# Meta tokens' squares from the copy loaded for the transposes, and the first row of products in the order of its operands

## The chip, the cores and the metric

The kernel runs on one core of a Trainium2 chip. TensorE (PE) multiplies: a matmul first loads a block of stationary operand (PEld in the profile, one LDWEIGHTS), then streams the columns of the moving operand past it and adds into a PSUM bank. VectorE (DVE) and ScalarE (ACT) do elementwise work, GpSimd (POOL) fills constants and issues a few DMAs, SyncE (SP) issues most DMAs. The metric is the device time of one execution in microseconds. The kernel before takes 1206.83 us, the median of three runs from 1205.95 to 1206.94.

## The reference, cut to what matters

```python
meta_b = jnp.broadcast_to(meta[None], (B, N_META, D_MODEL))     # 16 x 2048
h = jnp.concatenate([meta_b, x], axis=1)                        # 272 tokens
u = rms_norm(h, g_pre_mix[l])        # h / sqrt(mean(h*h) + eps) * g, token by token
proj = u @ w_in[l]                   # 2048 x 7168, split into z_pool, v, g, gate_a, gate_b
# pooling of z_pool, gated causal convolution of v and g, gates, w_o, second norm,
# w_up, relu squared, w_down, third norm
return h[:, N_META:]
```

The 272 tokens are 16 meta tokens ahead of 256 tokens of x. Each token's row is scaled by the root of the mean of its 2048 squares. The kernel multiplies the unscaled rows by the weights and brings the scale in afterwards, so the sums of squares are needed only when the first products are evacuated.

## The kernel before, in words

Everything is float32. To keep that precision, each operand is split into a high part in a rounded format of 4 bytes (fp32r) and a low part, the remainder in the same format; a product is the sum of high times high, high times low and low times high. ACT writes the high parts (L259, L1011, L1397), DVE the low parts (L262, L1016, L1402). Weights come as chunks of 128 partitions by 2048 columns into a raw buffer of 8192 bytes per partition, three in rotation, and are split into the buffers `hi` and `lo`, three of each.

The stages, in the order of TensorE's work:

- **Opening** (to about 38 us): `meta` is loaded twice, once as `m_rows`, 128 rows of two pieces of 128 columns, for the transposes, and once as `m_in`, 16 rows of 2048, for the squares. The tokens are turned by TensorE (L378, L396) into `u`, 16 tiles (k) of 128 features by 272 tokens, high and low. As soon as a k is there, `product_of(k)` (L538) multiplies it into four accumulators, by `mm3` (L441, matmuls at L446): three matmuls of 272 columns for each accumulator, stationary `hi` or `lo`, moving `u`. `x_tile`, `row` and `squares_of` for later k are issued in between, by the loop at L558; this order is written by hand. `keep_warm` (L364) issues matmuls that nobody reads ahead of the first product.
- **The other products of `u` with `mm3`** (to 155 us): the rest of v and g, and z, also 272 columns.
- **Gates** (to 330 us): `block_t` (L712, matmuls at L717) with the roles exchanged: `u` from its 17th token on is stationary, `hi` and `lo` are streamed, 512 columns.
- **Group map, pool and conv outputs, w_o** (to 512 us): L446 with 256 columns, then L717 and L1055 with 512 streamed columns of weights.
- **MLP** (to the end): products up by `mm2` (L460): `mm2_high` (L451) streams 512 columns (the high and low parts of 256 tokens) of the activations, tile `m`, past a stationary `hi`; `mm2_low` (L457) streams 256 columns of `m` past a stationary `lo`. Products down (L1551) stream 512 columns of weights past stationary `forms`. The order in both w_o and the MLP is made by a planner (class Plan) from costs and due times.

**Where tiles lie.** Tiles come from pools that stand one behind the other in each partition: `const` (small constants, each rounded up to 32 bytes), `big` (named slots: a tile that asks for the tag of an earlier one shares its place, and slots stand in the order in which their tags are first asked for), `raws`, `parts` (the `hi` and `lo` buffers), `tmp`. The kernel places some tiles by units of `LINE`, 16 floats or 64 bytes: the tile `shift` of three LINEs in `const` (L302), the offset of one LINE at the head of `m` (L815) and of one of the two `forms` (L1292), and in `part_tile` (L227):

```python
place = 2 if standing and tag == "hi" else 1
shift = (place - 1 - 3 * KEYS.index(key)) % 4 * LINE
return room[:, shift:shift + CK * CW]
```

So every `hi` and `lo` starts at the same remainder of 256 bytes, except the `hi` of the products up, which starts one LINE (64 bytes) later. In `big` the tags are asked for in the order k8 (two slots), a, c, um, s1, s0. The slot of tag a holds first `m_in` and later the convolution's input (8 x 286 floats, 9152 bytes), the slot of tag um holds `u` and later `m`.

Of the kernel before, what the change touches and what calls it, by code (L numbers as in the profile page):

```python
# [8 lines left out]
F32 = mybir.dt.float32  # L9
F32R = mybir.dt.float32r  # L10
AF = mybir.ActivationFunctionType
ALU = mybir.AluOpType
PSUM = bass.MemoryType.PSUM

P = 128
CK = 4
# [84 lines left out]
def hybrid_block(ctx: ExitStack, tc: tile.TileContext, ins: dict, out: bass.AP):  # L101
    nc = tc.nc
    x = ins["x"][0]
    meta = ins["meta"]
    T, D = x.shape
    M = meta.shape[0]
    L = M + T
    NT = T // P
    KD = D // P
# [17 lines left out]
    const = ctx.enter_context(tc.tile_pool(name="const", bufs=1))  # L127
    big = ctx.enter_context(tc.tile_pool(name="big", bufs=1))
    raws = ctx.enter_context(tc.tile_pool(name="raws", bufs=3))
    parts = ctx.enter_context(tc.tile_pool(name="parts", bufs=1))  # L130
    tmp = ctx.enter_context(tc.tile_pool(name="tmp", bufs=2))
# [6 lines left out]
    def acc_tile(name):  # L138
        return psA.tile([P, CW], F32, tag="acc", name=name)
# [73 lines left out]
    opened = []  # L213
# [21 lines left out]
    def open_chunk(loads=None):  # L235

        n = at["n"]
        at["n"] += 1
        src, (rows, width) = stream[n]
        raw = raws.tile([P, CK * CW], F32, tag="raw", name=f"raw_{n}")  # L240
        hi, lo = (part_tile(tag, at["parts"], n in standing_chunks) for tag in ("hi", "lo"))
        at["parts"] += 1
        flat, (raw, hi, lo) = raw, (t.rearrange("p (k c) -> p k c", k=rows) for t in (raw, hi, lo))
        if n < FIRST:
            dst = raw.rearrange("p k (h c) -> p k h c", h=2)
            for load in loads or [(slice(i, i + 2), BOTH, nc.sync) for i in range(0, rows, 2)]:
                if callable(load):
                    load()
                    continue
                sl, halves_, queue = load  # L250
                for k in range(sl.start, sl.stop):
                    queue.dma_start(dst[:, k, halves_], src[:, k, halves_])
        else:
            nc.sync.dma_start(raw, src)
        pieces = rows if n < FIRST else 4 if n == FIRST else 1
        k = rows // pieces

        def high(sl, cs):
            nc.scalar.copy(hi[:, sl, cs], raw[:, sl, cs])  # L259

        def low(sl, cs):
            nc.vector.tensor_sub(lo[:, sl, cs], raw[:, sl, cs], f32(hi[:, sl, cs]))  # L262

        def piece(i, cs):
            def f():
                sl = slice(i * k, (i + 1) * k)
                high(sl, cs)
                low(sl, cs)
            return f
        todo = [piece(i, slice(0, width)) for i in range(pieces)]  # L270
        if n == 0:
            todo[:1] = [piece(0, slice(h * HALF_CW, (h + 1) * HALF_CW)) for h in range(2)]
        opened.append((hi, lo, todo, flat))
# [5 lines left out]
    def fetch(ahead=2):  # L279

        for c in range(ahead + 1):
            if c == len(opened) and at["n"] < len(stream):
                open_chunk()
            if c < len(opened):
                split_pieces(c)
        flush()
        return opened.pop(0)[:2]
# [13 lines left out]

    const.tile([P, 3 * LINE], F32, name="shift")  # L302
    x_in = big.tile([P, NT, D], F32, tag="k8", bufs=2, name="x_in")
    m_in = big.tile([M, D], F32, tag="a", name="m_in")
    xv = x.rearrange("(t p) d -> p t d", p=P)
    XB = D // CW

# [24 lines left out]
    def load_x(queue, b, ts=slice(0, NT), cs=(0, 2)):  # L332

        sl = slice(b * CW + cs[0] * CW // 2, b * CW + cs[1] * CW // 2)
        queue.dma_start(x_in[:, ts, sl], xv[:, ts, sl])

    m_rows = tmp.tile([P, M * KD // P, P], F32, tag="v", bufs=5, name="m_rows")
    nc.sync.dma_start(m_rows, meta.rearrange("m (k f) -> (m k) f", f=P).rearrange(  # L340
        "(h p) f -> p h f", p=P))
    pre_rows = load_rows(nc.scalar, "g_pre_mix")
# [7 lines left out]
    load_x(nc.sync, 1)  # L350
    open_chunk()
    load_x(nc.sync, 2)
    nc.sync.dma_start(m_in, meta)
    open_chunk()
    load_x(nc.sync, 3)
    other_rows = load_rows(nc.gpsimd, "pool_scale", "b_dw", "conv_ln_g", "conv_ln_b", "g_pre_mlp")
# [1 line left out]
    nc.gpsimd.dma_start(taps_in, w_dw)  # L358
    ssq = const.tile([P, NT + 1, 2], F32, name="ssq")
    nc.gpsimd.memset(ssq, 1.0)  # L360

    idle = acc_tile("idle")

    def keep_warm(n):  # L364
        for _ in range(n):
            nc.tensor.matmul(idle[:, :P], rb[:, :P], rb[:, :P], start=True, stop=True)

    keep_warm(7)

    u = big.tile([P, KD, 2, -(-L // (4 * LINE)) * 4 * LINE], F32R, tag="um", name="u")[:, :, :, :L]
# [19 lines left out]
    def x_tile(k):  # L392
        pt = misc_tile(f"xt_{k}")[:, :T]
        sl = slice(k * P, (k + 1) * P)
        for t in range(NT):
            nc.tensor.transpose(pt[:, t * P:(t + 1) * P], x_in[:, t, sl], ident)  # L396
        nc.scalar.activation(u[:, k, 0, M:], pt, AF.Copy, scale=col("g_pre_mix", k))
        nc.vector.scalar_tensor_tensor(
            u[:, k, 1, M:], pt, col("g_pre_mix", k), f32(u[:, k, 0, M:]),
            op0=ALU.mult, op1=ALU.subtract)  # L400

    def squares_of(t, b):

        sl = slice(b * D // 2, (b + 1) * D // 2)
        src, n = (x_in[:, t, sl], P) if t < NT else (m_in[:, sl], M)
        nc.scalar.activation(src, src, AF.Square, accum_out=ssq[:n, t, b:b + 1])

    def rsqrt(r, q, var):

# [31 lines left out]
    def mm3(acc, hi, lo, act, k, cs, first, last):  # L441


        off = act.shape[3] - acc.shape[1]
        for n, (w, a) in enumerate(((hi, 0), (hi, 1), (lo, 0))):
            nc.tensor.matmul(acc, w[:, k[0], cs], act[:, k[1], a, off:],  # L446
                             start=first and n == 0, stop=last and n == 2)
# [18 lines left out]
    def acc_tiles(name, n=CW // P):  # L466
        return [acc_tile(f"acc_{name}_{j}") for j in range(n)]
# [68 lines left out]
    accs = [acc[:, :L] for acc in acc_tiles("vg0")]  # L536

    def product_of(k):  # L538
        for j, acc in enumerate(accs):
            mm3(acc, *opened[k // CK][:2], u, (k % CK, k), slice(j * P, (j + 1) * P),  # L540
                k == 0, k == KD - 1)

    def row(k):
        opened[k // CK][2].pop(0)()

    def x_pair(k):

        x_tile(k)
        x_tile(k + 1)
# [4 lines left out]
    row(0)  # L554
    x_tile(1)
    row(1)
    keep_warm(6)
    for k in range(KD):  # L558
        product_of(k)
        if k % CK == CK - 1:  # L560
            open_chunk()
        if k in (0, 2):
            for kx in (k + 2, k + 3):
                x_tile(kx)
                row(kx)
        elif k % 2 == 0 and k + 3 < KD:
            x_pair(k + 2)
        elif k + 3 < KD and k > 1:
            row(k + 3)
            row(k + 4)  # L570
        squares = {4: (NT, 0), 6: (0, 0), 8: (1, 0), 10: (NT, 1)}
        if k in squares:
            squares_of(*squares[k])
        if k == KD - 5:
            row(KD)
    for _ in range(3):
        row(KD)
    for t in range(NT):
        squares_of(t, 1)
# [177 lines left out]
    hi, lo = fetch()  # L757
    for g in range(NG):
        for j in range(GK):
            q = g * GK + j  # L760
            acc = (acc_tile if q < KP - 2 else misc_tile)(f"acc_grp_{q}")[:, :T]
# [476 lines left out]
    accs = acc_tiles("up00")  # L1238
# [41 lines left out]
    hi, lo = fetch()  # L1280
# [459 lines left out]
    for e, cs in enumerate(col_halves):  # L1740
        for w, s in ends:
            h = AT[s][0]
# [53 lines left out]
```

## Time and profile before

| | |
|---|---|
| runs | 1205.95, 1206.94, 1206.83 us; median 1206.83 |
| the profiled execution | 1206.63 us, its span 1204.5 us |
| granted clock of TensorE, mean | 0.998 |
| PE busy | 1195.1 us (99% of the span), 6444 matmul records |
| PEld busy | 1038.0 us (86%) |
| DVE busy | 974.3 us (81%) |
| ACT busy | 625.2 us (52%) |
| POOL busy | 8.3 us |
| DMA | 238.40 MB, mean 198 GB/s |

The span runs from the first to the last instruction of the profiled execution; the 2.1 us by which its time exceeds the span lie around it. A row of a group says: line, engine, operation, out<-in by the program's names, shape and count, then busy time in us and the mean duration of one in ns. Matmuls are pipelined: the duration of one is longer than the distance from its start to the start of the next, and the next one's LDWEIGHTS runs beside it. A matmul of plain float32 stands in the trace as two records.

### The profile page before, as it was taken

Reading aid. Unit: us, or ns where it says so; the run is one execution under the profiler, and the core shown is the slowest. Engines: PE = TensorE matmul, PEld = TensorE weight load, DVE = VectorE, ACT = ScalarE, POOL = GpSimd, SP = SyncE. Lnnn points to the kernel's source line nnn. Section 1 sums busy time; section 2 is a strip of 40 time slices with the busy share of each in tenths; the row PEclk is TensorE's granted clock in tenths of the full one; section 3 lists DMA queues with packets and bytes.
Section 4 is the critical chain, followed back from the end, with each engine's and each line's share of the span. In section 5 each row is a group of like instructions: output and inputs, shape, how many; then the busy total and the mean of one; then the engine's idle time right before and its main releaser. Section 6 shows DMA issues by size and latency. Waiting matters only on the chain.

```text
span 1204.5 us, 15705 instructions
## 1 busy us (share of the span) xinstructions
PE 1195.1 (99%) x6444; PEld 1038.0 (86%) x6444; DVE 974.3 (81%) x1054; ACT 625.2 (52%) x633; POOL 8.3 (1%) x19
## 2 busy tenths in 40 slices
PE   9999999999999999999999999999999999999997
PEld 9999988888888888898888888888888888888886
DVE  5899978999676778678988878788878778788756
ACT  6533344443583455666555564564554555554543
POOL 1000000000000000000000000000000000000000
PEclk9999999999999999999999999999999999999999
DMA  9655555656557588546475675674764764755841
GB/s 293 210 177 179 188 193 180 205 181 203 177 172 280 174 264 260 174 167 218 143 242 175 186 233 160 196 250 140 244 200 155 262 197 152 245 175 172 278 145 70
DMA packets 162678, 238.40 MB, mean 198 GB/s; under 512 B 4161, under 2 KB 92417, under 8 KB 162080
## 3 DMA queue, kind: packets, MB, share of 16 engines
q1 hardware_dynamic: 160032, 230.77, 58.4%
q0 software_dynamic: 1680, 5.40, 1.7%
q10 hardware_dynamic: 896, 1.25, 0.3%
q8 instruction: 50, 0.82, 0.3%
q14 instruction: 20, 0.16, 0.0%
HBM read 235.30 MB, written 2.10 MB: 197 GB/s over the span
## 4 chain that ended last, share of the span: by engine, by line
PE 97%; DMA 2%; DVE 1%; ACT 0%; ACTq 0%; DVEq 0%; issue 0%
PE bank_u L451 18%; PE acc_gate L717 14%; PE acc_up L1551 14%; PE bank_u L457 9%; PE bank_a L1551 7%; PE o_c L1055 6%; PE bank_b L1551 5%; PE acc_z L446 4%; PE acc_co L717 4%; PE acc_po L717 4%; PE acc_v L446 3%; PE acc_g L446 3%; PE acc_up L451 1%; PE acc_vg L446 1%; PE bank_u L1551 1%; DMA x_in<-in_x_dram 1%
## 5 line engine op out<-in xcount | busy, mean ns | idle before, releaser
L451 PE MATMUL bank_u<-m,hi 128*128 128x512 f32 x960 | 329.9, 390 | 0.0
L457 PE MATMUL bank_u<-m,lo 128*128 128x256 f32 x960 | 265.5, 277 | 0.0
L259 ACT CAST hi<-raw 128x2048 fp32r<-128x2048 f32 (+2 forms) x94 | 151.0, 1619 | 191.6 <-PE acc_gate L717 67.7
L1402 DVE TENSOR_TENSOR lo<-raw_m,hi 128x2048 fp32r<-128x2048 f32 x85 | 194.5, 2290 | 59.4 <-ACT hi L1397 59.3
L1397 ACT CAST hi<-raw_m 128x2048 fp32r<-128x2048 f32 x85 | 162.4, 1911 | 138.1 <-PE bank_u L451 76.8
L262 DVE TENSOR_TENSOR lo<-raw,hi 128x2048 fp32r<-128x2048 f32 (+2 forms) x94 | 180.1, 1925 | 42.5 <-ACT hi L259 42.0
L451 PEld LDWEIGHTS bank_u<-m,hi 128*128 128x128 f32 x960 | 180.2, 188 | 37.9
L457 PEld LDWEIGHTS bank_u<-m,lo 128*128 128x128 f32 x960 | 180.3, 188 | 1.6
L717 PE MATMUL acc_gate<-hi,u 128*128 128x512 f32 x512 | 158.6, 390 | 0.0
L1551 PE MATMUL acc_up<-hi,forms 128*128 128x512 f32 x496 | 157.5, 389 | 0.0
L512 DVE SCALAR_TENSOR_TENSOR c<-a,taps,c 128x256 f32<-128x256 f32 x240 | 115.7, 484 | 6.8
L717 PEld LDWEIGHTS acc_gate<-hi,u 128*128 128x128 f32 x512 | 96.1, 188 | 19.9
L1551 PEld LDWEIGHTS acc_up<-hi,forms 128*128 128x128 f32 x496 | 93.1, 188 | 19.4
L717 PE MATMUL acc_gate<-lo,u 128*128 128x512 f32 x256 | 99.6, 389 | 0.0
L1551 PE MATMUL acc_up<-lo,forms 128*128 128x512 f32 x248 | 96.6, 389 | 0.0
L1402 DVE TENSOR_TENSOR lo<-raw_c,hi 128x2048 fp32r<-128x2048 f32 x29 | 66.4, 2290 | 20.9 <-ACT hi L1397 20.9
L1551 PE MATMUL bank_a<-hi,forms 128*128 128x512 f32 (+1 forms) x256 | 82.0, 383 | 0.0
L1397 ACT CAST hi<-raw_c 128x2048 fp32r<-128x2048 f32 x29 | 55.3, 1908 | 50.9 <-PE bank_u L451 27.9
L1402 DVE TENSOR_TENSOR lo<-raw_a,hi 128x2048 fp32r<-128x2048 f32 x29 | 66.4, 2290 | 17.6 <-ACT hi L1397 17.5
L1397 ACT CAST hi<-raw_a 128x2048 fp32r<-128x2048 f32 x29 | 55.4, 1910 | 42.4 <-PE bank_u L451 19.4
L1055 PE MATMUL o_c<-hi,m 128*128 128x512 f32 x208 | 65.6, 390 | 0.0
L1551 PE MATMUL bank_b<-hi,forms 128*128 128x512 f32 (+1 forms) x200 | 63.7, 382 | 0.0
(317 smaller groups left out, 1853.0 us busy)
## 6 DMA issues: line engine op xcount, KB each, us to landing
raw<-in_w_in_dram SPq DMA_DIRECT2D x52, 1024.0 KB, 5.1
raw_m<-in_w_down_dram SPq DMA_DIRECT2D x37, 1024.0 KB, 5.3
raw_m<-in_w_up_dram SPq DMA_DIRECT2D x33, 1024.0 KB, 6.1
raw_c<-in_w_down_dram SPq DMA_DIRECT2D x14, 1024.0 KB, 5.2
raw_a<-in_w_up_dram SPq DMA_DIRECT2D x13, 1024.0 KB, 6.0
raw_a<-in_w_down_dram SPq DMA_DIRECT2D x13, 1024.0 KB, 5.3
raw_c<-in_w_up_dram SPq DMA_DIRECT2D x12, 1024.0 KB, 5.8
raw_o<-in_w_o_dram SPq DMA_DIRECT2D x10, 1024.0 KB, 7.2
```

The costliest lines, as they stand in the source:

```text
L259: nc.scalar.copy(hi[:, sl, cs], raw[:, sl, cs])
L262: nc.vector.tensor_sub(lo[:, sl, cs], raw[:, sl, cs], f32(hi[:, sl, cs]))
L446: nc.tensor.matmul(acc, w[:, k[0], cs], act[:, k[1], a, off:], start=first and n == 0, stop=last and n == 2)
L451: nc.tensor.matmul(acc.rearrange("p (a t) -> p a t", a=2)[:, :, ts], hi[:, k[0], cs], act[:, k[1], :, off + ts.start:off + ts.stop], start ...
L457: nc.tensor.matmul(acc[:, :T], lo[:, k[0], cs], act[:, k[1], 0, off:], start=False, stop=stop, skip_group_check=True)
L512: nc.vector.scalar_tensor_tensor(c, conv["a"][:, q, i:i + T], taps[:, q, i:i + 1], c, op0=ALU.mult, op1=ALU.add)
L717: nc.tensor.matmul(acc, act(kk)[:, a_, ts_], w_[:, k, :], start=kk == 0 and n == 0, stop=kk == nk - 1 and n == 2)
L1055: nc.tensor.matmul(acc, form(k, a_), box[w_][:, k, :], start=start and k == 0 and n == 0, stop=stop and k == CK - 1 and n == 2, skip_group ...
L1397: nc.scalar.copy(box["flat"], raw)
L1402: nc.vector.tensor_sub(lo, raw, f32(box["flat"]))
L1551: nc.tensor.matmul(acc, forms[h][:, f, k, a_, :], box[w_][:, k, cs], start=start and k == 0 and n == 0, stop=stop and k == KH - 1 and n == ...
```

## The change

The second copy of `meta` goes: no tile `m_in`, no DMA for it, no two ACT squares over it (k = 4 and k = 10). In its place ACT squares the two 128-column pieces of `m_rows` early and sums each row (a row holds 128 of the 2048 features of one meta token) into `row_ssq`; POOL makes a mask `rows_of` that says which rows belong to which token; two matmuls on TensorE (`meta_squares`) add the rows of each token into a corner of the PSUM tile `idle`; and DVE copies those 16 sums into `ssq` at k = 1. `ssq`'s second column for the meta tokens is set to zero. `keep_warm` ahead of the first product goes from 6 to 3. In `product_of(0)` the twelve matmuls are issued operand by operand (high weights with high `u` for all four accumulators, then high with low, then low with high) instead of accumulator by accumulator.

```diff
     x_in = big.tile([P, NT, D], F32, tag="k8", bufs=2, name="x_in")
-    m_in = big.tile([M, D], F32, tag="a", name="m_in")
...
-    m_rows = tmp.tile([P, M * KD // P, P], F32, tag="v", bufs=5, name="m_rows")
+    RH = M * KD // P
+    m_rows = tmp.tile([P, RH, P], F32, tag="v", bufs=5, name="m_rows")
...
     load_x(nc.sync, 2)
-    nc.sync.dma_start(m_in, meta)
...
     nc.gpsimd.memset(ssq, 1.0)
+    nc.gpsimd.memset(ssq[:, NT, 1:], 0.0)
+
+    rows_of = const.tile([P, RH, M], F32, name="rows_of")
+    nc.gpsimd.memset(rows_of, 1.0)
+    for sign, base in ((1, 0), (-1, KD - 1)):
+        nc.gpsimd.affine_select(rows_of, rows_of, pattern=[[sign * P, RH], [-sign * KD, M]],
+                                compare_op=ALU.is_ge, fill=0.0, base=base,
+                                channel_multiplier=sign)
+    row_ssq = const.tile([P, RH], F32, name="row_ssq")
...
     keep_warm(7)
+    for h in range(RH):
+        nc.scalar.activation(tmp.tile([P, P], F32, tag="junk", bufs=1, name=f"sqm_{h}"), m_rows[:, h, :], AF.Square,
+                             accum_out=row_ssq[:, h:h + 1])
...
     def squares_of(t, b):
 
         sl = slice(b * D // 2, (b + 1) * D // 2)
-        src, n = (x_in[:, t, sl], P) if t < NT else (m_in[:, sl], M)
-        nc.scalar.activation(src, src, AF.Square, accum_out=ssq[:n, t, b:b + 1])
+        src = x_in[:, t, sl]
+        nc.scalar.activation(src, src, AF.Square, accum_out=ssq[:, t, b:b + 1])
...
     def product_of(k):
-        for j, acc in enumerate(accs):
-            mm3(acc, *opened[k // CK][:2], u, (k % CK, k), slice(j * P, (j + 1) * P),
-                k == 0, k == KD - 1)
+        hi, lo = opened[k // CK][:2]
+        if k:
+            for j, acc in enumerate(accs):
+                mm3(acc, hi, lo, u, (k % CK, k), slice(j * P, (j + 1) * P), False, k == KD - 1)
+            return
+        for n, (w, a) in enumerate(((hi, 0), (hi, 1), (lo, 0))):
+            for j, acc in enumerate(accs):
+                nc.tensor.matmul(acc, w[:, 0, j * P:(j + 1) * P], u[:, 0, a, :], start=n == 0,
+                                 stop=False)
+
+    def meta_squares():
+
+        tot = idle[:M, P:P + 1]
+        for h in range(RH):
+            nc.tensor.matmul(tot, rows_of[:, h, :], row_ssq[:, h:h + 1],
+                             start=h == 0, stop=h == RH - 1)
+        return tot
...
-    keep_warm(6)
+    keep_warm(3)
+    meta_tot = meta_squares()
...
-        squares = {4: (NT, 0), 6: (0, 0), 8: (1, 0), 10: (NT, 1)}
+        squares = {6: (0, 0), 8: (1, 0)}
         if k in squares:
             squares_of(*squares[k])
+        if k == 1:
+            nc.vector.tensor_copy(ssq[:M, NT, 0:1], meta_tot)
```

Two things follow from this for where tiles lie. `const` grows by `rows_of` (2 x 16 floats, 128 bytes) and `row_ssq` (2 floats, rounded up to 32 bytes), 160 bytes together, so all pools behind it start 160 bytes later. And tag a is first asked for only when the convolution's input is made, after c and um: its slot of 9152 bytes now stands behind um instead of ahead of c, and c and um (with `u` and `m`) move forward by 9152 - 160 = 8992 bytes. Start addresses per partition in the two programs:

| tile | before | after |
|---|---|---|
| `x_in`, first of `big` | 20544 | 20704 |
| `u`, later `m` (whose data start 64 further) | 70656 | 61664 |
| slot s1 (`forms_1`, whose data start 64 further) | 111616 | 111776 |
| slot s0 (`forms_0`) | 128064 | 128224 |
| first raw buffer | 144448 | 144608 |
| `lo`, first buffer | 169024 | 169184 |

## The prediction

> **What bounds the kernel now.** I read the page's busy times first, then the chain that ended last.
>
> ```profile
> PE 1195.1 (99%) x6444; PEld 1038.0 (86%) x6444; DVE 974.3 (81%) x1054; ACT 625.2 (52%) x633; POOL 8.3 (1%) x19
> ...
> PE 97%; DMA 2%; DVE 1%; ACT 0%; ACTq 0%; DVEq 0%; issue 0%
> ```
>
> TensorE is busy 99% of the span and carries 97% of the chain. So there are two ways to move the time: the few microseconds in which TensorE waits, and the pace at which its 6444 records follow each other. The chain in order of time gives the pace of long unbroken stretches:
>
> ```profile
> 107.99 47.36 PE acc_z L446 x384
> 155.35 144.17 PE acc_gate L717 x636
> ```
>
> A matmul of 272 columns follows the last after 47.36/384 = 123 ns, one of 512 after 227 ns. The groups kept apart by shape have their durations:
>
> ```profile
> L451 PE MATMUL bank_u<-m,hi 128*128 128x512 f32 x960 | 329.9, 390 | 0.0
> L457 PE MATMUL bank_u<-m,lo 128*128 128x256 f32 x960 | 265.5, 277 | 0.0
> ...
> L446 PE MATMUL acc_z<-u,hi 128*128 128x272 f32 x256 | 47.4, 286 | 0.0
> ...
> L446 PE MATMUL acc_grp<-d,hi 128*128 128x256 f32 x32 | 5.8, 283 | 0.0
> ```
>
> 286 - 123 = 163 ns, and for the gates 390 (the duration that the 512-column group above also has) - 227 = 163 ns: duration is pace plus a constant, so a nanosecond more of duration is one more of time. What stands out: 256 columns take 277 ns in the products up and 283 ns in the group map. The first products up, asked for line by line in short windows, show what decides:
>
> ```profile
> L451 PE MATMUL acc_up<-m,hi x16: 276/276/366, 519.1 to 520.9; 128*128 128x256 f32 x16
> L457 PE MATMUL acc_up<-m,lo x16: 282/283/283, 521.0 to 522.8; 128*128 128x256 f32 x16
> L451 PE MATMUL acc_up<-m,parts_up x16: 281/283/364, 523.3 to 525.2; 128*128 128x256 f32 x16
> L451 PE MATMUL acc_up<-m,parts_up x16: 279/279/362, 528.1 to 530.0; 128*128 128x256 f32 x16
> ```
>
> All four stream 256 columns of `m`, whose data start at 70720, remainder 64 of 256 bytes. I call *distance* the start of the stationary operand loaded meanwhile minus the start of the streamed one, modulo 256. In the first row `hi` has place 2, remainder 128: distance 64, 276 ns. Second: `lo` at 64: distance 0, 283. Third: `parts_up` in slot s0 (128064, remainder 64): distance 0, 283. Fourth: slot s1 (111616, remainder 0): distance 192, 279. In the group map `d` lies in a k8 slot (remainder 64 like `x_in`) and `hi` at 64: 0, and 283 again. So for 256 columns the distance is worth up to 7 ns a matmul.
>
> **The change part by part.**
>
> *Where tiles lie.* By the table of addresses, `hi` and `lo` with place 1 go from remainder 64 to 224, `u` from 0 to 224, the data of `m` from 64 to 32, the `hi` of products up from 128 to 32. The distances:
> - L446 with 272 columns (`u` streamed): 64 becomes 0.
> - `mm2_low` (then `hi` is loaded): 64 becomes 0.
> - `mm2_high` (then `lo` is loaded): 0 becomes 192.
> - gates and w_o (`hi`, `lo` streamed, `u` or `m` loaded): 0 becomes 64.
> - L1551, pool and conv outputs, group map: 0 stays 0.
>
> *mm2_low*: 960 x (283 - 277) = +5.8 us. The ends are 0 (the pace does not follow the address here) and +5.8.
>
> *272 columns*: 192 (vg) + 288 (v) + 288 (g) + 384 (z) = 1152 matmuls, for which no row has distance 0. Free of any loss, 256 columns take 276 ns; each further column costs (227 - 113)/256 = 0.44 ns (113 = 276 - 163), so 272 would take 283 and now lose 3. Ends: 283 (-3 ns, -3.5 us) and 286 + 7 = 293 (+8.1 us). I take the free 283 plus the 7 that distance 0 costs in the group map, the nearest row since it is the same helper: 290, +4 ns, +4.6 us.
>
> *mm2_high*: no row has 512 columns at distance 192. At 0 they take 390; at 64 they are seen only where a product down ends and `hi` of a product up is loaded:
>
> ```profile
> 573.59 0.39 PE L1551 MATMUL acc_up<-lo,forms 128*128 128x512 f32 x1
> 573.81 0.39 PE L1551 MATMUL acc_up<-hi,forms 128*128 128x512 f32 x1
> 574.04 0.40 PE L451 MATMUL bank_u<-m,hi 128*128 128x512 f32 x1
> ```
>
> The last L1551 before L451 lasts no longer than the one before. So 512 columns don't seem to feel the distance: 0 for `mm2_high`, gates and w_o. The other end for `mm2_high` comes from a stretch of the same addresses at a slower pace, against the rest of the stage:
>
> ```profile
> L451 PE MATMUL bank_u<-m,hi x31: 393/393/396, 543.2 to 553.7; 128*128 128x512 f32 x31
> ...
> L457 PE MATMUL bank_u<-m,lo x31: 281/281/281, 543.4 to 553.9; 128*128 128x256 f32 x31
> ...
> L451 PE MATMUL bank_u<-m,hi x876: 389/389/398, 599.9 to 1157.4; 128*128 128x512 f32 x176
> ...
> L457 PE MATMUL bank_u<-m,lo x877: 276/276/280, 599.8 to 1157.7; 128*128 128x256 f32 x176
> ```
>
> There 512 columns reach 396: 960 x (396 - 390) = +5.8 us. That the pace differs at equal addresses also says that it isn't the distance alone.
>
> *The offset itself*: all big tiles now start 32 bytes off the 64-byte grid. DVE and ACT already work on such a tile, `dm` (L643), in the slot of tag junk, which starts 32 off that grid:
>
> ```profile
> L1512 DVE TENSOR_TENSOR forms<-F_raw,forms 128x512 fp32r<-128x512 f32 x32 | 21.8, 685 | 0.0
> L1511 ACT CAST forms<-F_raw 128x512 fp32r<-128x512 f32 x32 | 19.5, 617 | 0.5
> ...
> L649 DVE TENSOR_TENSOR d<-dm,d 128x512 fp32r<-128x512 f32 x4 | 2.7, 684 | 0.0
> L646 ACT CAST d<-dm 128x512 fp32r<-128x512 f32 x4 | 2.4, 612 | 0.0
> ```
>
> 684 against 685 and 612 against 617 ns: nothing. TensorE has no such row; I take 0.
>
> *The opening*, from the timeline:
>
> ```profile
> 4.69 0.12 POOL L360 MEMSET ssq<- 128x6 f32 x1
> 5.71 0.47 ACT L397 ACTIVATE u<-xt,vecs 128x256 fp32r<-128x256 f32 x1 [1.99 <-PE xt L396]
> 5.80 1.50 PE L366 MATMUL idle<-rb 128*128 128x128 f32 x12
> 6.08 0.70 ACT L259 CAST hi<-raw 128x256 fp32r<-128x256 f32 x2
> 6.62 0.41 DVE L390 TENSOR_TENSOR u<-mg,u 128x256 fp32r<-128x256 f32 x1
> 6.95 0.76 DVE L262 TENSOR_TENSOR lo<-raw,hi 128x256 fp32r<-128x256 f32 x2
> 7.06 0.49 PE L446 MATMUL acc_vg<-u,hi 128*128 128x272 f32 x2
> 8.15 0.69 DVE L262 TENSOR_TENSOR lo<-raw,hi 128x512 fp32r<-128x512 f32 x1
> 8.66 0.35 SPq L353 DMA_DIRECT2D m_in<-in_meta_dram  x1
> 8.77 0.60 PE L396 MATMUL xt<-ident,x_in 128*128 128x128 f32 x4
> 9.12 0.50 PE L446 MATMUL acc_vg<-u,hi 128*128 128x272 f32 x2
> 17.42 1.06 ACT L406 ACTIVATE m_in<-m_in 16x1024 f32<-16x1024 f32 x1 [0.35 <-DMA m_in<-in_meta_dram]
> ```
>
> Row 0 now takes 7.06 to 8.77, since each accumulator waits for its low weights (ready at 7.71). In the new order four matmuls with the high `u` can start at 6.75 (three `keep_warm` fewer, 0.75 us, then some 0.2 us for the two mask products), four with the low `u` from 7.24, four with the low weights from 7.73: the next transposes start at 8.2 instead of 8.77. Row 1's low weights still come at 8.15 + 0.69 = 8.84, so its third matmul gains some 0.6 us (from 9.12 + 0.37). The two squares on ACT (some 0.5 us each) lie in the 1.99 us that it idles ahead of 5.71; with `m_rows` late they would delay `u` one for one. POOL's four extra steps (0.1 to 0.3 us each, from 4.81) end before 6; TensorE would wait for them if they took twice that. Out go 128 KB from SP's queue and ACT's square ahead of later weight rows. But the loads carry on as before:
>
> ```profile
> 8.00:10.00 2.00, 2.00 (x19) 2.00 (x18) 1.10 (x3) 0.94 (x3) 0.00 (x0) 1.00 1.04 289
> 10.00:15.00 5.00, 5.00 (x41) 4.89 (x41) 3.63 (x8) 3.34 (x9) 0.00 (x0) 1.00 1.11 355
> ```
>
> With the DMA share (next to last) at 1.04 to 1.11 a lead can be lost to the next late load. Ends: 0 and -1.1 us (0.6 plus the freed 0.5 us of transfer); I take -0.6. DVE's copy at k = 1 (some 0.2 us) lies in its idle time: 0, or 0.2.
>
> *Sum*: 5.8 + 4.6 + 0 - 0.6 = +9.8 us on the profiled 1206.63, which is 0.2 below the median 1206.83; against the median 1216.6.
>
> **The rivals.**
> 1. *Layout costs nothing, the opening alone counts*: 1206.2 us. For it: equal addresses show two paces in the products up. Against: four rows of distance 0 or 64 that agree to 1 ns. The Trainium skill, in "TensorE: Matmul & The Clock Gate", Part 2: What happens when you issue a matmul, has the next weights loaded through a read port of their own that takes nothing from the running matmul; by that rule no address matters and this rival's time would come out. The trace doesn't agree: 276 and 283 ns for the same instruction.
> 2. *512 columns pay too*: 5.8 us more, 1222.4, and with 272 columns at their upper end 1225.9. For it: the 396 ns; against: 390 and 389 wherever the distance is 0.
> 3. *Faster: distance 0 is the free one for 272 columns.* In the stages of L446 1152 x 3 ns = -3.5 us, with the opening 1202.7. It decides (below 1204.4) only if `mm2_low` loses less than 1.8 ns each. Against: 283 in the group map with the same helper.
> 4. *Half a 64-byte step costs TensorE itself*: at the same 7 ns on 6444 records, +45 us, 1251. No row for it.
>
> **How the numbers follow.** Some 0.2% (2.4 us) is what a measurement of this kernel can tell from no change. Chances: forecast 0.44 (range 1210 to 1220), rival 1 0.20, rival 2 0.20, rival 3 0.11, rival 4 0.05. Slower 0.44 + 0.20 + 0.05 = 0.69, same 0.20, faster 0.11. The range leaves out rivals 3 and 4: from 1204.5 to 1228.
>
> **What would show it.** L457 of `bank_u` at 283 instead of 277 ns; L446 `acc_z` at 290 instead of 286; L451, L717 and L1551 unchanged near 390; the second pair of transposes at 8.2 us; stage borders of the chain after 540 us drifting apart at some 5.8 us over the MLP. It is wrong if the 272- or 256-column rows keep their durations, if 512 columns change, or if TensorE waits for the mask or the row sums ahead of its first product.

## The result and the profile after

The changed kernel takes 1223.99 us (median of four runs, 1223.72 to 1224.1); the kernel before took 1206.88 us beside it (four runs, 1205.95 to 1207.15). The ratio is 1.0143, with a 95% interval from 1.0125 to 1.016: slower by 17.1 us. The profiled execution took 1224.02 us with a span of 1221.9 us and a mean granted clock of 0.998, as before; the difference of the spans is 17.4 us, and it is these that the trace can divide.

In the changed kernel the lines lie further down: L446 is now L457, L451 L462, L457 L468, L717 L745, L1055 L1083 and L1551 L1579. (So "L457" is `mm2_low` in rows of before and `mm3` in rows of after.)

The page of after, busy times and shares of the chain that ended last:

```profile
PE 1212.1 (99%) x6442; PEld 1043.3 (85%) x6442; DVE 975.6 (80%) x1055; ACT 625.6 (51%) x633; POOL 8.8 (1%) x23
...
PE 98%; DVE 1%; DMA 0%; ACT 0%; SPq 0%; issue 0%; DVEq 0%; ACTq 0%
```

TensorE is busy for 17.0 us more, and DVE and ACT for 1.3 and 0.4 us. So hardly any wait was added (the span less TensorE's busy time is 9.4 us before and 9.8 after); TensorE's own work takes longer, with practically the same number of records (6442 against 6444). Where it does is told by the first matmul of each stage, in us from the start of the span:

| stretch, from the first matmul of one tile to that of the next | before | after | difference |
|---|---|---|---|
| start to `acc_v` (opening) | 34.81 | 35.03 | +0.22 |
| `acc_v` to `acc_gate` (272 columns: v, g, z) | 120.38 | 122.31 | +1.93 |
| `acc_gate` to `acc_grp` (gates) | 175.02 | 180.06 | +5.04 |
| `acc_grp` to `o_c` (group map, pool and conv outputs) | 95.55 | 95.54 | 0 |
| `o_c` to `acc_up` (w_o) | 86.08 | 88.30 | +2.22 |
| `acc_up` to `bank_u` | 25.73 | 25.78 | +0.05 |
| `bank_u` to the end (MLP) | 666.95 | 674.93 | +7.98 |

The differences add up to 17.4 us. The chain in order of time shows the same as a pace. Of before, two stretches that the prediction did not show:

```profile
336.14 43.55 PE acc_po L717 x192
...
483.94 25.84 PE o_c L1055 x114
```

Of after, these and the two shown of before:

```profile
109.37 48.13 PE acc_z L457 x384
157.50 148.40 PE acc_gate L745 x636
...
343.33 43.55 PE acc_po L745 x192
...
492.58 26.60 PE o_c L1083 x114
```

A matmul of 272 columns now follows the last after 48.13/384 = 125.3 ns instead of 123.3, a gate's after 148.40/636 = 233.3 instead of 226.7, one of w_o after 26.60/114 = 233.3 instead of 226.7. The pool outputs, which stream 512 columns of the same buffers through the same line as the gates, take 43.55 us in both. They don't load `u`.

The groups kept apart by shape, of after:

```profile
L462 PE MATMUL bank_u<-m,hi 128*128 128x512 f32 x960 | 338.2, 396 | 0.0
L468 PE MATMUL bank_u<-m,lo 128*128 128x256 f32 x960 | 268.5, 280 | 0.0
L745 PE MATMUL acc_gate<-hi,u 128*128 128x512 f32 x512 | 161.9, 396 | 0.0
L1579 PE MATMUL acc_up<-hi,forms 128*128 128x512 f32 x496 | 157.4, 389 | 0.0
L457 PE MATMUL acc_z<-u,hi 128*128 128x272 f32 x256 | 48.2, 288 | 0.0
...
L457 PE MATMUL acc_grp<-d,hi 128*128 128x256 f32 x32 | 5.8, 283 | 0.0
```

and of before, the two that the prediction took by their likeness to `bank_u`:

```profile
L717 PE MATMUL acc_gate<-hi,u 128*128 128x512 f32 x512 | 158.6, 390 | 0.0
L1551 PE MATMUL acc_up<-hi,forms 128*128 128x512 f32 x496 | 157.5, 389 | 0.0
```

`mm2_high` went from 390 to 396 ns, `mm2_low` from 277 to 280, the gates from 390 to 396, `acc_z` from 286 to 288. The products down stay at 389 and the group map at 283: of these rows the two whose distance the change leaves at 0. The operands of all six rows now lie 32 bytes off the 64-byte grid. The mean from one start to the next, which is what adds up to time, went from 227.5 to 233.4 ns for `mm2_high` and from 113.9 to 116.7 for `mm2_low`.

The opening of after, from the timeline (start, duration, engine, line):

```profile
5.18 0.50 POOL L365 TENSOR_SCALAR_AFFINE_SELECT rows_of<-rows_of 128x32 f32<-128x32 f32 x2
...
6.32 0.25 PE L564 MATMUL idle<-row_ssq,rows_of 128*16 128x1 f32 x4
...
6.50 1.27 PE L557 MATMUL acc_vg<-u,hi 128*128 128x272 f32 x8
...
7.61 0.66 PE L557 MATMUL acc_vg<-u,lo 128*128 128x272 f32 x4
...
8.11 0.60 PE L407 MATMUL xt<-ident,x_in 128*128 128x128 f32 x4
...
8.30 0.62 ACT L259 CAST hi<-raw 128x512 fp32r<-128x512 f32 x1 [1.43 <-DMA raw<-in_w_in_dram]
...
8.97 0.51 PE L457 MATMUL acc_vg<-u,hi 128*128 128x272 f32 x2 [0.26 <-ACT hi L259]
```

The mask is ready at 5.68 and TensorE uses it at 6.32, without a wait. The first row runs operand by operand and the second pair of transposes starts at 8.11 instead of 8.77. But row 1's weights are cast only at 8.30, after ACT waited 1.43 us for their DMA, and TensorE waits for that cast: the lead ends there.

DVE and ACT work at their old pace 32 bytes off the grid (685 and 617 ns before):

```profile
L1540 DVE TENSOR_TENSOR forms<-F_raw,forms 128x512 fp32r<-128x512 f32 x32 | 21.8, 686 | 0.0
L1539 ACT CAST forms<-F_raw 128x512 fp32r<-128x512 f32 x32 | 19.6, 619 | 0.5
```

### The profile page after: what moved, and what is told of

Read it like the earlier page. It is cut to its first block, busy times and chain, and to the rows that moved or that the text cites. A ratio compares the mean times of both kernels' runs of the same rounds, so it can differ in the third digit from the quotient of the medians.

```text
span 1221.9 us, 15706 instructions
## 1 busy us (share of the span) xinstructions
PE 1212.1 (99%) x6442; PEld 1043.3 (85%) x6442; DVE 975.6 (80%) x1055; ACT 625.6 (51%) x633; POOL 8.8 (1%) x23
## 4 chain that ended last, share of the span: by engine, by line
PE 98%; DVE 1%; DMA 0%; ACT 0%; SPq 0%; issue 0%; DVEq 0%; ACTq 0%
PE bank_u L462 18%; PE acc_gate L745 15%; PE acc_up L1579 14%; PE bank_u L468 9%; PE bank_a L1579 7%; PE o_c L1083 6%; PE bank_b L1579 5%; PE acc_z L457 4%; PE acc_co L745 4%; PE acc_po L745 4%; PE acc_v L457 3%; PE acc_g L457 3%; PE acc_vg L457 2%; PE acc_up L462 1%; PE bank_u L1579 1%; PE o_a L1083 1%
## 5 line engine op out<-in xcount | busy, mean ns | idle before, releaser
L462 PE MATMUL bank_u<-m,hi 128*128 128x512 f32 x960 | 338.2, 396 | 0.0
L468 PE MATMUL bank_u<-m,lo 128*128 128x256 f32 x960 | 268.5, 280 | 0.0
L462 PEld LDWEIGHTS bank_u<-m,hi 128*128 128x128 f32 x960 | 180.5, 188 | 42.4
L468 PEld LDWEIGHTS bank_u<-m,lo 128*128 128x128 f32 x960 | 181.3, 189 | 1.6
L745 PE MATMUL acc_gate<-hi,u 128*128 128x512 f32 x512 | 161.9, 396 | 0.0
L1579 PE MATMUL acc_up<-hi,forms 128*128 128x512 f32 x496 | 157.4, 389 | 0.0
L745 PEld LDWEIGHTS acc_gate<-hi,u 128*128 128x128 f32 x512 | 96.3, 188 | 23.1
L1579 PEld LDWEIGHTS acc_up<-hi,forms 128*128 128x128 f32 x496 | 93.1, 188 | 19.4
L745 PE MATMUL acc_gate<-lo,u 128*128 128x512 f32 x256 | 101.3, 396 | 0.0
L1579 PE MATMUL acc_up<-lo,forms 128*128 128x512 f32 x248 | 96.5, 389 | 0.0
L1579 PE MATMUL bank_a<-hi,forms 128*128 128x512 f32 (+1 forms) x256 | 81.9, 383 | 0.0
L1083 PE MATMUL o_c<-hi,m 128*128 128x512 f32 x208 | 66.8, 396 | 0.0
L1579 PE MATMUL bank_b<-hi,forms 128*128 128x512 f32 (+1 forms) x200 | 63.6, 381 | 0.0
```

What stands on the lines that cost most here:

```text
L462: nc.tensor.matmul(acc.rearrange("p (a t) -> p a t", a=2)[:, :, ts], hi[:, k[0], cs], act[:, k[1], :, off + ts.start:off + ts.stop], start ...
L468: nc.tensor.matmul(acc[:, :T], lo[:, k[0], cs], act[:, k[1], 0, off:], start=False, stop=stop, skip_group_check=True)
L745: nc.tensor.matmul(acc, act(kk)[:, a_, ts_], w_[:, k, :], start=kk == 0 and n == 0, stop=kk == nk - 1 and n == 2)
L1083: nc.tensor.matmul(acc, form(k, a_), box[w_][:, k, :], start=start and k == 0 and n == 0, stop=stop and k == CK - 1 and n == 2, skip_group ...
L1579: nc.tensor.matmul(acc, forms[h][:, f, k, a_, :], box[w_][:, k, cs], start=start and k == 0 and n == 0, stop=stop and k == KH - 1 and n == ...
```

## Experiments

After this the theory was: the whole loss comes from where `u` and `m` lie relative to what is loaded beside them, which the tag a asked for late has moved; the opening's edits as such cost nothing. Its rivals: the 32 bytes off the grid cost TensorE time, or something in the opening (order, mask, queues) does. Kernels e1 to e4 ran together, beside a kernel before of 1206.72 us; e5 to e8 beside 1206.61; e9 to e11 beside 1206.66. The rows of e2, e3, e6, e9, e10 and e11 have line numbers that are one higher than in after, those of e7 and e8 three: L463 and L465 are `mm2_high` there.

### On the grid again: e1_on_grid

The tile that sets the offset gives up the 160 bytes that the two new constants take, so that every big tile is back on the 64-byte grid. The distances stay those of after.

```diff
-    const.tile([P, 3 * LINE], F32, name="shift")
+    const.tile([P, 8], F32, name="shift")
```

> The changed kernel with the tile shift cut from 48 to 8 floats, which takes back the 160 bytes: all big tiles on the 64-byte grid again, and hi, lo, forms and raw at the addresses of before; u and m stay moved (remainder 64 instead of 0), so every distance is that of the changed kernel. Theory D (the distance between the operand loaded and the operand streamed sets the pace): no change against the changed kernel, 1223 to 1225 us; gates, mm2_high and w_o at 396 ns, mm2_low 280, acc_z 288. Theory O (the half step off the 64-byte grid sets it): back to 1206 to 1208 us, gates and mm2_high at 390.

Measured: 1223.37 us, ratio 1.0140 (1.0124 to 1.0155). By shape:

```profile
L462 PE MATMUL bank_u<-m,hi 128*128 128x512 f32 x960 | 338.2, 396 | 0.0
L468 PE MATMUL bank_u<-m,lo 128*128 128x256 f32 x960 | 268.5, 280 | 0.0
L745 PE MATMUL acc_gate<-hi,u 128*128 128x512 f32 x512 | 161.9, 396 | 0.0
```

All three rows are those of after to the digit. The offset from the grid isn't the cause.

### The old order of slots: e2_old_slots

A tile that nobody uses asks for tag a where `m_in` did, so that c and um stand behind it again. The distances are those of before, the 32 bytes off the grid stay.

```diff
     x_in = big.tile([P, NT, D], F32, tag="k8", bufs=2, name="x_in")
+    big.tile([M, D], F32, tag="a", name="room_a")
```

> The changed kernel with the tag a asked for at its old place by a tile that nothing uses, so the slots of big stand in the order of before; everything still starts 160 bytes later, half a step off the 64-byte grid, and all distances are those of before. Theory D: 1206 to 1207.5 us, gates, mm2_high and w_o at 390 ns, mm2_low 277, acc_z 286. Theory O: 1223 to 1225 us with 396 ns in gates and mm2_high.

Measured: 1206.20 us, ratio 0.9995 (0.9986 to 1.0005).

```profile
L463 PE MATMUL bank_u<-m,hi 128*128 128x512 f32 x960 | 329.9, 390 | 0.0
L469 PE MATMUL bank_u<-m,lo 128*128 128x256 f32 x960 | 265.5, 277 | 0.0
L746 PE MATMUL acc_gate<-hi,u 128*128 128x512 f32 x512 | 158.6, 390 | 0.0
```

One unused tile takes back the whole loss, and all groups have the durations of before. With e1 this settles that the order of the slots makes the loss, and not the grid. That order moves the slots of tags a, c and um together; e7 and e8 below move `u` and `m` alone.

### Both together: e3_both_back, and again e11_both_back_again

Both edits: every address of before, the opening of after.

> Both edits: the addresses of before with the changed opening, so only the opening is left of the change. Theory of the prediction: 0 to -1.1 us against before, 1206.3 us. Rival (the late landing of weight row 1, 8.30 us instead of 7.50 in the changed kernel, is made by the change in the opening itself): +0.2 to +0.8 us, 1207 to 1207.7.

Measured: 1206.38 us, ratio 0.9997 (0.9988 to 1.0007). Against e2 the half step of 32 bytes off the grid is worth 0.18 us the wrong way round, that is nothing. The same kernel was run a second time, to see whether the opening gains anything:

> e3_both_back once more, in five rounds: the changed opening with the addresses of before. By the stage borders of its profile (gates begin 0.9 us earlier than before, the span is 0.7 us shorter) 0.3 to 0.9 us faster than before, ratio 0.9993 to 0.9998; if that lead was of one execution alone, ratio 1.0000 within 0.0003.

Measured: 1206.20 us, ratio 0.9996 (0.9988 to 1.0005). The three kernels that have the new opening and the old distances lie 0.34 to 0.52 us below before, and each interval holds 1. A gain of the opening of 0.6 us is neither shown nor excluded.

### The layout alone: e4_layout_alone

The other way round: the kernel before, with its old opening, and only the addresses of after (160 bytes more in `const`, and c and um asked for ahead of tag a).

```diff
-    const.tile([P, 3 * LINE], F32, name="shift")
+    const.tile([P, 3 * LINE + 40], F32, name="shift")
     x_in = big.tile([P, NT, D], F32, tag="k8", bufs=2, name="x_in")
+    taps_in = big.tile([TAPS, CC], F32, tag="c", name="taps_in")
+    u = big.tile([P, KD, 2, -(-L // (4 * LINE)) * 4 * LINE], F32R, tag="um", name="u")[:, :, :, :L]
     m_in = big.tile([M, D], F32, tag="a", name="m_in")
```

> The kernel before with nothing but the addresses of the changed kernel: shift grown by 40 floats, and taps_in and u allocated ahead of m_in, so that slot a stands behind um. Theory D and theory O both: the whole loss comes with the addresses, 1223.5 to 1225 us, that is +17 us; rival (the opening makes part of it, the main stages the rest): 1222.5 or less.

Measured: 1224.09 us, ratio 1.0145 (1.013 to 1.016), the loss of the whole change, with the second copy of `meta`, its squares and the old order of products still in place.

### The order of the first row alone: e5_order_alone

The kernel before with only the new `product_of`.

```diff
-        for j, acc in enumerate(accs):
-            mm3(acc, *opened[k // CK][:2], u, (k % CK, k), slice(j * P, (j + 1) * P),
-                k == 0, k == KD - 1)
+        hi, lo = opened[k // CK][:2]
+        if k:
...
+        for n, (w, a) in enumerate(((hi, 0), (hi, 1), (lo, 0))):
+            for j, acc in enumerate(accs):
+                nc.tensor.matmul(acc, w[:, 0, j * P:(j + 1) * P], u[:, 0, a, :], start=n == 0,
+                                 stop=False)
```

> The kernel before with nothing but the new order of the first row's twelve matmuls. It shows which part of the opening makes the lead: with both parts and the old addresses the second pair of transposes starts at 8.33 us and acc_v at 33.91, before at 8.77 and 34.81. If the order makes it, the pair starts by 8.45 and acc_v by 34.2; if the three keep_warm fewer and the missing second load make it, both stay within 0.2 us of before. The time stays within 1 us of before either way.

Measured, in a single run: 1206.11 us; the second pair of transposes at 8.68 us, `acc_v` at 34.28. That decides nothing. The start of `acc_v` lies at 34.81 in before, 34.23 in e1, 34.37 in e2, 33.91 in e3, 34.92 in e4 and 34.69 in e11, so the same opening (e3 and e11) moves by 0.8 us between two executions, as the first weights land earlier or later. Which part of the opening, if any, makes a lead stays open.

### One distance at a time in the products up: e6, e9, e10

The prediction had split the products up into `mm2_high`, to cost nothing at 192, and `mm2_low`, to cost 6 ns at 0. With the changed opening, all addresses of before and only the places of `hi` and `lo` of the products up changed, each distance was moved alone. In e6 `hi` goes back to the place of `lo`: `mm2_high` stays at 0, `mm2_low` goes to 0 as in after.

```diff
-        place = 2 if standing and tag == "hi" else 1
+        place = 1
```

> The addresses of before with the changed opening, and place 1 for every hi: in the products up mm2_low goes from distance 64 to 0 and mm2_high stays at 0, so mm2_low's price stands alone (in the changed kernel mm2_high went to 192 as well). By the prediction, 283 ns as in the group map: +5.8 us, 1212 us. By the changed kernel's mean, 280 ns: +2.9 us, 1209.3 us. Rival: mm2_low loses only when mm2_high does, 277 ns and 1206.4 us.

Measured: 1217.57 us, ratio 1.0092 (1.0075 to 1.0109).

```profile
L463 PE MATMUL bank_u<-m,hi 128*128 128x512 f32 x960 | 340.7, 398 | 0.0
L469 PE MATMUL bank_u<-m,lo 128*128 128x256 f32 x960 | 269.4, 281 | 0.0
```

The matmul whose own distance did not change, `mm2_high`, went from 390 to 398 ns, more than the one whose distance did. In e9 `lo` is moved instead: `mm2_high` to 192, `mm2_low` stays at 64.

```diff
-        place = 2 if standing and tag == "hi" else 1
+        place = (2 if tag == "hi" else 0) if standing else 1
```

> The addresses of before with the changed opening, and lo of the products up at place 0: mm2_high at distance 192, as in the changed kernel, and mm2_low at 64, as before. Theory E (a loss belongs to one load against one stream, each matmul by its own distance): mm2_high 396 ns as in the changed kernel, mm2_low 277, +5.8 us, 1212 us. Theory F (the pair decides: a load that meets its stream badly shows in the matmul after it, so the 396 in the changed kernel came from mm2_low at 0, as the 236 ns pace of mm2_high at its old distance in e6_low_alone says): mm2_high 390, 1206 to 1208 us, and any loss shows in mm2_low.

Measured: 1216.73 us, ratio 1.0081 (1.0068 to 1.0095).

```profile
L463 PE MATMUL bank_u<-m,hi 128*128 128x512 f32 x960 | 339.9, 396 | 0.0
L469 PE MATMUL bank_u<-m,lo 128*128 128x256 f32 x960 | 270.9, 282 | 0.0
```

Here too both matmuls lose. In e10 `mm2_high` goes to 64 and `mm2_low` stays at 64 (`place = 2 if standing else 1`):

> The same with lo of the products up at place 2: mm2_high and mm2_low both at distance 64. Theory E: by the 396 of the gates at 64, +5.8 us, 1212 us. Theory F: between no change and what e8_um_192 showed with mm2_high at 64 and mm2_low at 128 (pair 347 ns against 341), 1206 to 1212 us, the loss in mm2_low.

Measured: 1219.03 us, ratio 1.0101 (1.0085 to 1.0116).

```profile
L463 PE MATMUL bank_u<-m,hi 128*128 128x512 f32 x960 | 340.9, 397 | 0.0
L469 PE MATMUL bank_u<-m,lo 128*128 128x256 f32 x960 | 269.8, 281 | 0.0
```

All three came out slower than any theory had put them: e6 at 1217.57 us against 1212 at most, e9 at 1216.73 against 1212, e10 at 1219.03 against 1212.

### Other places for `u` and `m`: e7_um_128 and e8_um_192

With the addresses of before, `u` and `m` moved by 128 or 192 bytes and every other tile left at its remainder (an unused tile of 2 or 3 LINEs ahead of `u`, one of 2 or 1 behind it, so that all behind moves by 256). The edit of e7:

```diff
+    big.tile([P, 2 * LINE], F32, tag="pad0", name="pad0")
     u = big.tile([P, KD, 2, -(-L // (4 * LINE)) * 4 * LINE], F32R, tag="um", name="u")[:, :, :, :L]
+    big.tile([P, 2 * LINE], F32, tag="pad1", name="pad1")
```

> The addresses of before with the changed opening, but u and m 128 bytes further (every other tile keeps its remainder): gates and w_o at distance 128, mm2_high at 128, mm2_low and the 272 columns at 192. If any distance but 0 costs 512 columns 6 ns, gates, w_o and mm2_high stand at 396 and the time is 1219 to 1226 us; if the loss falls off with the distance (half at 128 of what it is at 64), at 393 and 1212 to 1217.

> The same with u and m 192 bytes further: gates and w_o at distance 192, mm2_high at 64, mm2_low and the 272 columns at 128. If any distance but 0 costs 512 columns 6 ns: gates, w_o and mm2_high 396, 1219 to 1226 us. If only 64 is bad for gates and only 192 for mm2_high: 390, and 1205 to 1212 us. The 272 columns at 128 show whether some distance is free for them (283 ns, -3.5 us).

Measured, in one run each: 1221.64 and 1217.27 us. The time of e7 is that of the theory that any distance but 0 costs, yet only the gates (395 ns) and w_o grow as it says, while `mm2_high` stays at 389; e8 lies between the times of its two theories. The chain of e7 (gates at distance 128, `acc_z` at 192):

```profile
109.75 48.64 PE acc_z L460 x384
158.39 147.78 PE acc_gate L748 x636
```

and of e8 (gates at 192, `acc_z` at 128):

```profile
109.91 48.64 PE acc_z L460 x384
158.55 145.60 PE acc_gate L748 x636
```

The gates take 232.4 and 228.9 ns each, `acc_z` 126.7 in both. The mean time from one start to the next, in ns, for the matmuls of the high weights with both parts of `u`, by one kernel for each distance (the chain above takes in the low weights as well):

| distance | 0 | 64 | 128 | 192 |
|---|---|---|---|---|
| gates, 512 columns | 227.5 (before) | 234.1 (after) | 233.1 (e7) | 228.8 (e8) |
| `acc_z`, 272 columns | 125.2 (after) | 123.2 (before) | 126.5 (e8) | 126.5 (e7) |

and a pair of `mm2_high` and `mm2_low`, by their two distances:

| kernel | `mm2_high` at | `mm2_low` at | `mm2_high` | `mm2_low` | pair |
|---|---|---|---|---|---|
| before | 0 | 64 | 227.5 | 113.9 | 341.4 |
| after | 192 | 0 | 233.4 | 116.7 | 350.1 |
| e6 | 0 | 0 | 235.9 | 116.8 | 352.7 |
| e9 | 192 | 64 | 232.9 | 119.3 | 352.2 |
| e10 | 64 | 64 | 234.7 | 118.3 | 353.0 |
| e7 | 128 | 192 | 228.4 | 118.3 | 346.7 |
| e8 | 64 | 128 | 228.2 | 118.5 | 346.7 |

So a price for each matmul by its own distance doesn't exist here. Moving `mm2_low` alone costs 11.3 ns a pair, moving `mm2_high` alone 10.8, and both at once, as the change does, only 8.7. `mm2_high` at 64 takes 228.2 in e8 and 234.7 in e10. Of all that was tried the placement of before is the best in the 272 columns, the gates, w_o and the MLP. What in the machine makes the pace depend on these remainders is not shown by any of the runs.

## Why the prediction was right or wrong

The forecast was 1216.6 us in a range from 1204.5 to 1228, slower; 1223.99 was measured. The sign and the cause were right: a tile that moves in memory, and not the work that the change takes out or adds. The size, +9.8 us against +17.1, was not: the time lies outside the 1210 to 1220 us that the forecast itself had, and inside the whole range only because that took in rival 2. Terms were off in both directions, and one of the prediction's own signs of being wrong, that 512 columns change, came true.

| term | forecast, us | measured, us | from |
|---|---|---|---|
| `mm2_low` | +5.8 | +2.7 | 960 x (116.7 - 113.9) |
| `mm2_high` | 0 | +5.7 | 960 x (233.4 - 227.5) |
| 272 columns | +4.6 | +2.3 | 1152 x 2 ns; of it 1.93 in v, g and z |
| gates | 0 | +5.0 | the stretch |
| w_o | 0 | +2.2 | the stretch |
| opening | -0.6 | -0.2 | +0.22, less the 0.4 that its 192 matmuls of 272 columns lose |
| offset of 32 bytes | 0 | 0 | e1 against after, e2 against e3 |

They add up to 17.7; the MLP as a whole lost 0.4 less than its two terms say.

*"512 columns don't seem to feel the distance."* This is the step that failed, and it was worth 12.9 us (`mm2_high`, gates and w_o). It rested on one hand-over around 573.8 us, where the last product down meets distance 64, and it read the duration of that matmul alone. The trace of before has the loss one row further on, in the first `mm2_high` behind the hand-over; in lines that round to 10 ns it hardly shows. In the view of the line by itself (shortest, median and longest duration in ns, then first and last start), first the one behind the hand-over, then the 15 that follow:

```profile
L451 PE MATMUL bank_u<-m,hi x1: 397/397/397, 574.0 to 574.0; 128*128 128x512 f32 x1
...
L451 PE MATMUL bank_u<-m,hi x15: 389/389/389, 574.4 to 579.2; 128*128 128x512 f32 x15
```

All 42 hand-overs from products down to products up in before have 397 or 398 ns there, and so do the 42 of e3. In e6, which differs from e3 only in the place of `hi` of the products up, the hand-over is at distance 0, and all 42 have 389:

```profile
L463 PE MATMUL bank_u<-m,hi x1: 389/389/389, 573.3 to 573.3; 128*128 128x512 f32 x1
```

So even one encounter of 512 columns with distance 64 costs, some 8 ns, but the matmul behind it shows it. This also fits e6, where `mm2_low` is moved and `mm2_high` grows; alone it doesn't explain e9, where `mm2_high` is moved and both grow.

The other end of the prediction for `mm2_high`, +5.8 us, came out to 0.1 us. It was drawn from a stretch of before at distance 0, however, and no run shows that the same thing is behind both, so the agreement counts as luck. Rival 2, at 1222.4 to 1225.9 us with a chance of 0.20, has the right time and the right idea that 512 columns pay. But it priced `mm2_high` alone: the 7.2 us of the gates and w_o are missing in it, and `mm2_low` and the 272 columns, 5.4 us too high, make up for most of them.

*`mm2_low` at 283 ns.* It became 280. The row of 283 was of 256-column matmuls that follow each other; in the products up they alternate with 512 columns, and e6 shows that the two share the loss: with `mm2_low` alone moved to 0 it takes 281 and `mm2_high` 398. The pair, which the prediction would have put at +6 ns there, lost 11.3. The mis-step is related to the one above: a price per matmul was carried from one sequence to another.

*272 columns, 290 ns.* The row went from 286 to 288. The direction (distance 64 is better than 0) was right, so rival 3 is out, but 7 ns from the group map was too much: 2 ns at 0, and 3.3 at 128 and 192. That 64 is not free is not shown; it was the best of four.

*The Trainium skill's rule* in "TensorE: Matmul & The Clock Gate", Part 2: What happens when you issue a matmul, that loading the next weights takes nothing from the running matmul, and with it rival 1, is not borne out for 512 columns either: the gates last 390 ns in e2 and 396 in after, two kernels in which `hi` and `lo` lie at the same remainders and only `u` at another. Whether it is read bandwidth that the load takes, no run shows. The 1206.2 us that rival 1 gave were reached, but by e2, which puts the addresses back.

*The offset itself*, rival 4: nothing, as taken. e1 and after have the same rows, and in after the products down (389 ns) and the group map (283) keep their pace off the grid. DVE and ACT likewise, 686 against 685 and 619 against 617 ns.

*The opening.* Its steps came as written: transposes at 8.11 us (8.2 forecast), the mask and the row sums ready in time, DVE's copy hidden. Its worth was not -0.6 in the profiled execution, since the next weights were late, as the prediction allowed; beyond the scatter of the openings nothing is shown.

## What to carry to other kernels

When an edit frees, adds or reorders a tile, list the addresses of all operands of TensorE in both programs before pricing the edit itself: here one request for a tag, which came later, cost 17 us, and one line that asks for it early (e2) takes it all back. Read the pace of a long steady row, from the chain or from start to start. Where only a hand-over between two stages shows an address, read the matmul behind it too, in single ns. And where two shapes alternate, price the pair and not the matmul. If the placement was tuned, pin it, so that a later edit of a small constant or a tag can't move it.

## What was not expected of the hardware

With a granted clock of 0.998 or 0.999 in all profiled executions, the pace of matmuls in this float format depends on the difference of two start addresses, of the operand loaded and of the one streamed: by up to 7 ns in 227 (512 columns) and 3 in 123 (272 columns). It is the difference that counts, since e1 and after lie 160 bytes apart in all these tiles and have the same rows. Only steps of 64 bytes were tried, and that the period is 256 was not tested by itself. The order of the four distances differs with the shape: in the gates, where 512 columns follow 512, 0 is the best and 64 the worst; for 272 columns 64 is the best.

In an alternating sequence the loss shows up in both matmuls, also in the one whose own distance stayed, and two moves together cost less (8.7 ns a pair) than either alone (10.8 and 11.3). The means hide patterns: in after `mm2_low` takes mostly 274 and 285 ns by turns, at one and the same distance.

Before itself has two paces at the same addresses. The first products up of the MLP, from 537.6 to 560 us, run at 393 to 397 ns (the 473 stands behind matmuls of another kind); the prediction looked at 11 us of them:

```profile
L451 PE MATMUL bank_u<-m,hi x64: 393/396/473, 537.6 to 560.1; 128*128 128x512 f32 x64
```

They follow other products up. Those from 574 us on stand behind products down and run at 389 but for the first behind each hand-over. So what ran ahead may matter as well as the addresses; no run here tests it.

32 bytes off the 64-byte grid cost nothing on TensorE, VectorE or ScalarE.
